# A 64 KB copy of a constant tile on SyncE's queue in front of gamma's row, in an RMSNorm-SiLU kernel

## The chip, the cores and the metric

The kernel runs on one core of one Trainium2 chip. The metric is the device time of one execution in microseconds (us), as the median of several runs. A profile is one execution recorded instruction by instruction. In it PE is the matrix engine (TensorE), DVE is VectorE, ACT is ScalarE, POOL is GpSimd, and SP is SyncE, which here does nothing but issue transfers. An engine name with a q behind it (ACTq, SPq) is that engine's sequencer issuing transfers.

## The reference

```
x: float32 [8, 1024, 2048], gamma: float32 [2048], eps = 1e-5
rms = sqrt(mean(x ** 2, axis=-1, keepdims=True) + eps)
out = gamma * x / rms
return out * (1 / (1 + exp(-out)))        # float32
```

Each of the 8192 rows of 2048 numbers is divided by its root mean square, multiplied by gamma, and put through SiLU. 67.1 MB are read and 67.1 MB are written.

## The kernel before

**Blocks.** The 8192 rows are cut into 16 blocks of 512. A block is one SBUF tile `xt` of 128 partitions with J = 4 rows each, 8192 numbers or 32 KB in a partition, 4 MB in all. Six such tiles exist (BUFS = 6), and the work is done in place: load, multiply, SiLU, store, all in the same tile. So load b can be issued only when the store of block b-6 has landed.

**Queues.** Every load of `xt` is issued by ACT (`load`, L54). Every store is issued by SP (`store`, L102). So is gamma's row (L110). In the transfer view ACT's queue is called q10 and SP's queue q1. A transfer of a 4 MB tile is 128 packets of 32 KB, one for a partition, over the 16 DMA engines, that is 8 on each, and 16 packets of 4 bytes, one for each engine, that report the end (the semaphore).

**Setup.** The order is written out by hand (`manual_schedule`), and each engine works through its own list in that order:

- ACT issues load(0); then does a Square of one column of `ones` (L109, it brings in an activation table); then issues load(1); then copies one column of `junk_v` (L116), and only then issues load(2) to load(5). L116 reads `junk_v` and, as the profile shows, comes after DVE's copy of L115.
- DVE sets `ones` (a constant tile of 128x128) and `eps_t`, then copies the broadcast gamma from PSUM to `g` (L115), and only then begins on block 0.
- SP issues the load of gamma's 8 KB into partition 0 of `g` (L110).
- PE multiplies a row of `ones` with gamma's row (L113), which puts gamma in all 128 partitions of `junk_v` in PSUM.

**Steady work.** For each block ACT and DVE share the sums of squares (`squares_scalar` L65, `squares_vector` L73), ACT takes the root (L82), DVE the reciprocal (L87). DVE then multiplies each row by it and by `g` (`multiply`, L92), and ACT applies SiLU in two halves (L98) and SP stores the block. Loads 6 to 15 are issued by ACT inside `squares_scalar`: load b+3 comes right after the first Square of block b+1.

Of the kernel before, what the change touches and what calls it, by code (L numbers as in the profile page):

```python
# [1 line left out]

# [4 lines left out]

ACT = mybir.ActivationFunctionType
ALU = mybir.AluOpType


@with_exitstack
def kernel(
    ctx: ExitStack,
    tc: tile.TileContext,
    x: bass.AP,
    gamma: bass.AP,
    eps: bass.AP,
    out: bass.AP,
):  # L20

    nc = tc.nc
    P = nc.NUM_PARTITIONS
    f32 = mybir.dt.float32
    x2 = x.flatten_outer_dims()
    o2 = out.flatten_outer_dims()  # L30
    n, d = x2.shape
    J = 4
    BUFS = 6
    nblk = n // (P * J)
    xb = x2.rearrange("(b p j) d -> b p (j d)", p=P, j=J)
    ob = o2.rearrange("(b p j) d -> b p (j d)", p=P, j=J)

    singles = ctx.enter_context(tc.tile_pool(name="singles", bufs=1))
    pool = ctx.enter_context(tc.tile_pool(name="pool", bufs=BUFS))
    small = ctx.enter_context(tc.tile_pool(name="small", bufs=2))  # L40
    psum = ctx.enter_context(tc.tile_pool(name="psum", bufs=1, space=bass.MemoryType.PSUM))

    Q = 4
    w = d // Q
    g = singles.tile([P, d], f32)
    eps_t = singles.tile([P, 1], f32)
    ones = singles.tile([P, P], f32)
    junk_a = psum.tile([P, d], f32, name="junk_a")
    junk_v = psum.tile([P, d], f32, name="junk_v")
    blocks, sss, rmss, rstds = {}, {}, {}, {}  # L50

    def load(b):
        xt = pool.tile([P, J * d], f32, name="xt")
        nc.scalar.dma_start(out=xt, in_=xb[b])  # L54
        blocks[b] = xt

    def row(b, j):
        return blocks[b][:, j * d:(j + 1) * d]

    def squares_scalar(b, loads=()):  # L60


        sss[b] = small.tile([P, J], f32, name="ss")
        for j in range(share(b)):
            nc.scalar.activation(out=junk_a, in_=row(b, j), func=ACT.Square,  # L65
                                 accum_out=sss[b][:, j:j + 1])
            if j == 0:
                for s in loads:
                    load(s)

    def squares_vector(b):
        for j in range(share(b), J):
            nc.vector.tensor_tensor_reduce(  # L73
                out=junk_v, in0=row(b, j), in1=row(b, j), scale=1.0, scalar=0.0,
                op0=ALU.mult, op1=ALU.add, accum_out=sss[b][:, j:j + 1])

    def share(b):
        return 1 if 4 <= b <= 12 and b % 2 == 0 else 2

    def root(b):  # L80
        rms = small.tile([P, J], f32, name="rms")
        nc.scalar.activation(out=rms, in_=sss.pop(b), func=ACT.Sqrt, scale=1.0 / d, bias=eps_t)  # L82
        rmss[b] = rms

    def invert(b):
        rstd = small.tile([P, J], f32, name="rstd")
        nc.vector.reciprocal(out=rstd, in_=rmss.pop(b))  # L87
        rstds[b] = rstd

    def multiply(b):  # L90
        for j in range(J):
            nc.vector.scalar_tensor_tensor(out=row(b, j), in0=row(b, j), scalar=rstds[b][:, j:j + 1],  # L92
                                           in1=g, op0=ALU.mult, op1=ALU.mult)

    def silu(b):
        for h in range(0, J, 2):
            cols = slice(h * d, (h + 2) * d)
            nc.scalar.activation(out=blocks[b][:, cols], in_=blocks[b][:, cols], func=ACT.Silu)  # L98
        store(b)

    def store(b):
        nc.sync.dma_start(out=ob[b], in_=blocks[b])  # L102

    with tc.manual_schedule():

        load(0)
        nc.vector.memset(ones, 1.0)  # L107
        nc.vector.memset(eps_t, float(eps))
        nc.scalar.activation(out=junk_a[:, 0:1], in_=ones[:, 0:1], func=ACT.Square)  # L109
        nc.sync.dma_start(out=g[0:1, :], in_=bass.AP(tensor=gamma.tensor, offset=gamma.offset, ap=[[d, 1], [1, d]]))  # L110
        for c in range(Q):
            cols = slice(c * w, (c + 1) * w)
            nc.tensor.matmul(junk_v[:, cols], ones[0:1, :], g[0:1, cols], start=True, stop=True)  # L113
        load(1)
        nc.vector.tensor_copy(out=g, in_=junk_v)  # L115
        nc.scalar.copy(out=junk_a[:, 0:1], in_=junk_v[:, d - 1:d])  # L116
        for b in range(2, BUFS):
            load(b)

        last = nblk - 1
        SOON = 3
        squares_scalar(0)
        squares_vector(0)
        root(0)
        invert(0)
        for b in range(last):
            loads = [b + 3] if BUFS <= b + 3 < nblk else []
            if b < SOON:  # L130
                multiply(b)
                squares_scalar(b + 1, loads)
                silu(b)
                squares_vector(b + 1)
                root(b + 1)
            elif b < last - 1:
                squares_scalar(b + 1, loads)
                squares_vector(b + 1)
                root(b + 1)
                multiply(b)  # L140
                silu(b)
            else:
                multiply(b)
                squares_scalar(b + 1)
                silu(b)
                squares_vector(b + 1)
                root(b + 1)
            if b + 1 < last:
                invert(b + 1)


        for j in range(J):
            if j == J // 2:
                invert(last)
            nc.vector.tensor_mul(out=row(last, j), in0=row(last, j), in1=g)  # L155
        for j in range(J):
            nc.scalar.activation(out=row(last, j), in_=row(last, j), func=ACT.Silu,  # L157
                                 scale=rstds[last][:, j:j + 1])
        store(last)


# [1 line left out]
_INS = ['x', 'gamma', 'eps']  # L163
_OUTS = [((8, 1024, 2048), 'float32')]

_NUMBERS = {'eps': 9.999999747378752e-06}


# [26 lines left out]
```

## Time and profile before

| what | value |
|---|---|
| median of 3 runs | 316.87 us (316.86 to 317.06) |
| span of the profiled execution | 315.1 us |
| moved by the DMA engines | 134.24 MB, 426 GB/s over the span |
| DVE busy | 235.3 us (75%) |
| ACT busy | 213.9 us (68%) |
| PE busy | 7.2 us (2%) |
| DMA share of the chain that ended last | 68% |

The span runs from the first to the last instruction. The device time of the runs holds it and what lies around it, 316.87 - 315.1 = 1.8 us.

### The profile page before, as it was taken

The numbers are of one execution on the slowest core, as the hardware profiler recorded it, in microseconds if no ns is written. First come the engines' busy times: TensorE is split into PE (matmuls) and PEld (weight loads), VectorE is DVE, ScalarE is ACT, GpSimd is POOL, SyncE is SP. The second block draws the span as 40 slices with busy tenths as digits, with TensorE's granted clock in tenths as the row PEclk, the third lists the DMA queues.
The fourth block names the chain that finished last, engine by engine and source line by source line (L and its number), as shares of the span: only waits on it lengthen the run. The fifth ranks groups of instructions, "written<-read, shape, count | busy, mean of one in ns | idle before, by whom it ended". The sixth has DMA issues, their size and how long they took to land.

```text
span 315.1 us, 439 instructions
## 1 busy us (share of the span) xinstructions
PE 7.2 (2%) x8; PEld 2.5 (1%) x8; DVE 235.3 (75%) x157; ACT 213.9 (68%) x137; POOL 0.2 (0%) x4
## 2 busy tenths in 40 slices
PE   6200000000000000000000000000000000000000
PEld 2000000000000000000000000000000000000000
DVE  0679697979895695957969489593995939999600
ACT  1269998972799258682687827877278768779910
POOL 0000000000000000000000000000000000000000
DMA  8999999999999999999999999999999999999997
GB/s 334 412 453 416 383 458 408 462 403 462 403 459 408 454 412 458 408 462 403 462 403 462 408 458 408 458 408 458 416 449 416 449 416 449 428 437 428 437 428 308
DMA packets 4613, 134.24 MB, mean 426 GB/s; under 512 B 514, under 2 KB 514, under 8 KB 514
## 3 DMA queue, kind: packets, MB, share of 16 engines
q10 hardware_dynamic: 2304, 67.11, 49.8%
q1 hardware_dynamic: 2306, 67.12, 49.3%
q14 instruction: 3, 0.02, 0.0%
HBM read 67.12 MB, written 67.11 MB: 426 GB/s over the span
## 4 chain that ended last, share of the span: by engine, by line
DMA 68%; DVE 14%; ACT 11%; issue 1%; ACTq 1%; DVEq 0%
DMA xt<-in_x_dram 68%; DVE xt L92 9%; DVE junk_v L73 5%; ACT xt L98 4%; ACT junk_a L65 3%; ACT xt L157 2%; ACT L82 1%; ACTq L190 1%; ACT L157 0%; ACT L98 0%; ACT rms L82 0%; DVE ss L73 0%; ACTq L54 0%; DVE rstd L87 0%; ACT L109 0%
## 5 line engine op out<-in xcount | busy, mean ns | idle before, releaser
L92 DVE SCALAR_TENSOR_TENSOR xt<-xt,rstd,g 128x2048 f32<-128x2048 f32 x60 | 137.0, 2346 | 0.1
L98 ACT ACTIVATE xt<-xt 128x4096 f32<-128x4096 f32 x30 | 108.3, 3615 | 27.4 <-DVE xt L92 27.4
L73 DVE CUSTOM_DVE_ANT_0 junk_v<-xt 128x2048 f32<-128x2048 f32 x37 | 85.1, 2299 | 42.9 <-DMA xt<-in_x_dram 42.2
L65 ACT ACTIVATE junk_a<-xt 128x2048 f32<-128x2048 f32 x27 | 50.7, 1876 | 16.1 <-DMA xt<-in_x_dram 14.0
L82 ACT ACT_TABLE_LOAD x15 | 19.2, 1283 | 26.6 <-DVE ss L73 26.5
L98 ACT ACT_TABLE_LOAD x14 | 18.0, 1283 | 0.2
L115 DVE COPY g<-junk_v 128x2048 f32<-128x2048 f32 x1 | 2.3, 2292 | 9.0 <-PE junk_v L113 9.0
L87 DVE RECIPROCAL rstd<-rms 128x4 f32<-128x4 f32 x16 | 2.7, 172 | 8.4 <-ACT rms L82 8.4
L155 DVE TENSOR_TENSOR xt<-xt,g 128x2048 f32<-128x2048 f32 x4 | 8.9, 2277 | 0.0
L82 ACT ACTIVATE rms<-ss,eps_t 128x4 f32<-128x4 f32 x16 | 4.8, 297 | 5.7 <-DVE ss L73 5.5
L157 ACT ACTIVATE xt<-xt,rstd 128x2048 f32<-128x2048 f32 x4 | 7.7, 1991 | 0.0
L113 PE MATMUL junk_v<-g,ones 1*128 1x512 f32 x8 | 7.2, 1072 | 2.8 <-DMA g<-in_gamma_dram 2.8
L116 ACT COPY junk_a<-junk_v 128x1 f32<-128x1 f32 x1 | 0.1, 144 | 9.8 <-DVE g L115 9.8
L73 DVE DVE_READ_ACCUMULATOR2_ANT ss<- 128x1 f32 x37 | 5.2, 141 | 0.0
L65 ACT ACTIVATION_READ_ACCUMULATOR junk_a<-xt 128x1 f32 x27 | 5.0, 186 | 0.0
L113 PEld LDWEIGHTS junk_v<-g,ones 1*128 1x128 f32 x8 | 2.5, 325 | 5.9 <-issue 5.9
L109 ACT ACT_TABLE_LOAD x1 | 1.3, 1283 | 1.1 <-PEq L176 1.1
L157 ACT ACT_TABLE_LOAD x1 | 1.3, 1283 | 0.0
L107 DVE MEMSET ones<- 128x128 f32 x1 | 0.2, 165 | 0.8 <-PEq L176 0.8
L109 ACT ACTIVATE junk_a<-ones 128x1 f32<-128x1 f32 x1 | 0.2, 174 | 0.0
L176 POOL MEMSET const-bfloat16-1.0<- 128x1 bf16 x1 | 0.1, 103 | 0.0
L176 POOL MEMSET const-uint8-127<- 128x1 uint8 x1 | 0.1, 102 | 0.0
(3 smaller groups left out, 0.3 us busy)
## 6 DMA issues: line engine op xcount, KB each, us to landing
xt<-in_x_dram ACTq DMA_DIRECT2D x16, 4096.0 KB, 38.7
out_dram<-xt SPq DMA_DIRECT2D x16, 4096.0 KB, 29.0
g<-in_gamma_dram SPq DMA_DIRECT2D x1, 8.0 KB
```

Source lines behind the costliest of these rows:

```text
L65: nc.scalar.activation(out=junk_a, in_=row(b, j), func=ACT.Square, accum_out=sss[b][:, j:j + 1])
L73: nc.vector.tensor_tensor_reduce(out=junk_v, in0=row(b, j), in1=row(b, j), scale=1.0, scalar=0.0, op0=ALU.mult, op1=ALU.add, accum_out=sss ...
L82: nc.scalar.activation(out=rms, in_=sss.pop(b), func=ACT.Sqrt, scale=1.0 / d, bias=eps_t)
L87: nc.vector.reciprocal(out=rstd, in_=rmss.pop(b))
L92: nc.vector.scalar_tensor_tensor(out=row(b, j), in0=row(b, j), scalar=rstds[b][:, j:j + 1], in1=g, op0=ALU.mult, op1=ALU.mult)
L98: nc.scalar.activation(out=blocks[b][:, cols], in_=blocks[b][:, cols], func=ACT.Silu)
L109: nc.scalar.activation(out=junk_a[:, 0:1], in_=ones[:, 0:1], func=ACT.Square)
L113: nc.tensor.matmul(junk_v[:, cols], ones[0:1, :], g[0:1, cols], start=True, stop=True)
L115: nc.vector.tensor_copy(out=g, in_=junk_v)
L155: nc.vector.tensor_mul(out=row(last, j), in0=row(last, j), in1=g)
L157: nc.scalar.activation(out=row(last, j), in_=row(last, j), func=ACT.Silu, scale=rstds[last][:, j:j + 1])
L190: with _tile.TileContext(nc) as tc:
```

## The change

One more SBUF tile of 128x128 float32, `spare`, and one more transfer. SP sends all of `ones`, 512 bytes in each of 128 partitions (64 KB), to `spare`, in front of gamma's row. Nothing reads `spare`. The transfer reads `ones`, which DVE sets, so SP waits for that before it issues it, and gamma's row is issued behind it by the same engine on the same queue. All other engines keep their lists of instructions.

```diff
     ones = singles.tile([P, P], f32)
+    spare = singles.tile([P, P], f32)
...
         nc.scalar.activation(out=junk_a[:, 0:1], in_=ones[:, 0:1], func=ACT.Square)
+        nc.sync.dma_start(out=spare, in_=ones)
         nc.sync.dma_start(out=g[0:1, :], in_=bass.AP(tensor=gamma.tensor, offset=gamma.offset, ap=[[d, 1], [1, d]]))
```

## The prediction

> **What bounds the kernel now.** I read the page's slices and queues first, then busy time by stretch.
>
> ```profile
> DMA  8999999999999999999999999999999999999997
> q10 hardware_dynamic: 2304, 67.11, 49.8%
> q1 hardware_dynamic: 2306, 67.12, 49.3%
> HBM read 67.12 MB, written 67.11 MB: 426 GB/s over the span
> 4.00:35.00 31.00, 5.94 (x7) 1.75 (x6) 20.95 (x14) 17.99 (x14) 0.00 (x0) 1.00 0.99 427
> 36.00:40.00 4.00, 0.00 (x0) 0.00 (x0) 3.17 (x3) 3.96 (x5) 0.00 (x0) 1.00 1.09 377
> 40.00:280.00 240.00, 0.00 (x0) 0.00 (x0) 194.53 (x129) 168.71 (x105) 0.00 (x0) 1.00 1.00 433
> ```
>
> The DMA engines are full in every slice but the first and last. The last two columns of the stretches are the DMA share and GB/s: 1.00 and 433 from 40 to 280 us. At 433 GB/s the 134.24 MB need 310.0 us of the 315.1; start, end and small dents are the rest. DVE is busy 194.5 of those 240 us, ACT 168.7. So transfers bound the kernel, and a time in which both queues are empty is lost for good. A block of 4.19 MB takes 4.19 MB / 433 GB/s = 9.7 us, so each engine's packet of 32 KB, eight to a block, takes 1.21 us.
>
> Next the timeline of the first 15 us, for what the new transfer stands in front of.
>
> ```profile
> 0.73 0.38 ACTq L54 DMA_DIRECT2D xt<-in_x_dram  x1
> 0.73 0.33 SPq L110 DMA_DIRECT2D g<-in_gamma_dram  x1
> 0.82 0.17 DVE L107 MEMSET ones<- 128x128 f32 x1 [0.82 <-PEq L176]
> 1.21 0.39 ACTq L54 DMA_DIRECT2D xt<-in_x_dram  x1
> ...
> 2.78 7.16 PE L113 MATMUL junk_v<-g,ones 1*128 1x512 f32 x8 [2.78 <-DMA g<-in_gamma_dram]
> ...
> 9.97 2.29 DVE L115 COPY g<-junk_v 128x2048 f32<-128x2048 f32 x1 [8.98 <-PE junk_v L113]
> 12.36 0.14 ACT L116 COPY junk_a<-junk_v 128x1 f32<-128x1 f32 x1 [9.75 <-DVE g L115]
> 12.38 1.81 ACTq L54 DMA_DIRECT2D xt<-in_x_dram  x4
> ```
>
> Gamma lands at 2.78. Then come eight matmuls (7.16), DVE's copy (2.29) and ACT's column, and only behind that does ACT issue loads 2 to 5, at 12.38: 9.6 us after gamma's landing. Until then loads 0 and 1 alone feed the engines. The chain of waits has load 1 from 1.21 for 21.45 us, so it lands at 22.66.
>
> **The slack.** Load 2 follows load 1 without a gap now, so it lands at 22.66 + 9.7 = 32.4. If it is issued when the queue is empty, it lands as load 0 does: the landings of L54 begin with 12.2 us from issue (shown below), so at gamma + 9.6 + 12.2. The two meet at gamma = 32.4 - 21.8 = 10.6 us. Before that a late gamma costs nothing, since loads 0 and 1 cover it; after it each us of gamma is a us in which no queue has work. The delay of the span is gamma's landing less 10.6.
>
> **How two queues share the engines.** The trace of before does not show a 64 KB copy, but shows SP's queue starting beside loads in flight: store 0, issued at 35.18. Transfer views of 35.2 to 39.55, of 40 to 45.6 and of 56.5 to 59.1 us (queue: packets, MB, share of 16 engines' time), and the landings of L54:
>
> ```profile
> q10 hardware_dynamic: 43, 1.41, 95.1%
> ...
> q1 hardware_dynamic: 34, 1.11, 46.0%
> q10 hardware_dynamic: 32, 1.05, 43.3%
> ...
> DMA packets 52, 1.18 MB, mean 454 GB/s; under 512 B 16, under 2 KB 16, under 8 KB 16
> q10 hardware_dynamic: 32, 1.05, 93.3%
> q1 hardware_dynamic: 20, 0.13, 12.0%
> ...
> DMA to landing us min/median/max: 12.2/38.7/71.5
> ```
>
> First, up to 39.55, 4.4 us after the issue, SP's queue moved nothing (q1 is not in the answer). Second, once both run, they take turns one packet each: 34 against 32. Third, a turn is a packet, whatever its size: around 58 us store 0 ends, and its 16 semaphore packets of 4 bytes come up; in that stretch the loads moved 32 packets and SP's queue these 16 and 4 large ones, 93.3% of the time against 12.0%. A packet of 4 bytes cost SP's queue its whole turn.
>
> The Trainium skill, page DMA: Bandwidth & Descriptors, section Queues, rings and completion order, says that an engine drains a whole packet from one ring before it switches, typically 9 to 17 descriptors. If its descriptors are these records, that is against the 34 to 32 above. By the rule a load's 8 and one would go as a lump; it is priced as the second rival below, from rows.
>
> **The change part by part.**
>
> *The wait for `ones`.* SP issued gamma at 0.73; now it waits for the memset, 0.82 + 0.17 = 0.99, and issues `spare` at some 1.05 and gamma 0.33 to 0.39 later (the issue rows). That is 0.7 us on gamma, hidden many times over by the 10.6 - 2.8 = 7.8 us of slack. On SP only gamma is queued behind it; the first store comes at 35 us.
>
> *The order at the engines.* Now gamma's packet goes out at 1.64 (0.9 us after its issue) and no load's packet stands in front of it. After the change load 0's packets do: they begin at about the same 1.7 to 2.8, and `spare` is issued 0.3 us behind load 0. The first turn of SP's queue, F, is bounded by two rows: below by gamma's own 0.9 us and one load packet in progress (the first ones, cold, take 1.8 us): 1.7 + 1.8 = 3.5; above by store 0's 4.4 us and the rest of a packet: 1.05 + 4.4 + 0.5 = 6.0. I take 5.5, near store 0, since it is the row with loads in flight.
>
> *The turns.* 128 packets of 512 bytes over 16 engines are 8 on each, and one semaphore packet; behind them on one engine stand gamma's 8 KB and its semaphore: 11 packets, 10 turns of the loads between them. Load 0 has some 5 packets left at F, then its own semaphore (a turn of almost nothing), then load 1's: 9 turns of 1.21 = 10.9 us. SP's own packets: eight of 512 bytes and gamma's. No row has 512 bytes; between the next ones, 4 bytes (under 0.02 us) and 8 KB (0.7 us cold), I put 0.05 each, so 0.4, and 0.5 for gamma: 0.9 together. From the last packet to the matmul 0.4 (now 1.64 + 0.7 = 2.34, and the matmul at 2.78). Gamma lands at 5.5 + 10.9 + 0.9 + 0.4 = 17.7 instead of 2.8.
>
> A table of the same page, section Bandwidth, gives 64 KB in one transfer 0.95 us when it is alone (issued from GpSimd); by it gamma would land some 2 us late and the sum would be zero. No run here shows that figure; loads in flight are what it leaves out.
>
> *What follows.* Delay = 17.7 - 10.6 = 7.1 us. Loads 2 to 5 go out at 27.3; from about 22 to 29 nothing moves. The 64 KB themselves, 8 x 0.05 = 0.4 us for each engine, lie in front of that gap and so cost nothing more.
>
> *Knock-on.* DVE and ACT start block 0 only behind `g` too, so all of their first blocks come some 14.9 us later, less the 2.75 us that ACT now waits for load 1. First store about 47 to 48, load 6 (now issued at 66.7) at about 79. Does a queue run dry? Load 5 now lands at 13.7 + 71.5 = 85.2, so load 6 has 18.5 us to spare. In the new order loads 2 to 5 run alone from 28.5 to about 52 (2.4 blocks of 9.7), the other 1.6 blocks at half pace, 31 us, to about 83: load 6 comes before that, and stores 0 to 2 are waiting beside it in any case. DVE has (240 - 194.5)/240 = 19% in hand to catch up. At the end stores are queued (store 15 lands 13.4 us after its issue, not 9.7 + start), so the transfers stay the bound. No further loss and no recovery: lost transfer time does not come back at 433 GB/s. 315.1 + 7.1 = 322.2 of span; with the 1.8 us around it, and 316.87 as the median, 324.0.
>
> Ends: F = 3.5 gives gamma 15.7 and +5.1 (322.0). F = 6.0, a tenth full turn and 0.1 us for each small packet (+0.4) give 19.8, +9.2 (326.1). A gain out of these terms is excluded: each only delays.
>
> **The rivals.**
>
> *Small packets share a turn: no change (0.10).* If the engine drains a queue's small packets together, gamma lands at 5.5 + 0.5 + 1.2 + 0.5 + 1.2 + 0.4 = 9.3, before the 10.6 that decides. Load 2 is queued in time, and only 0.4 us of packets are added: 317.3, which is within 0.2% (0.6 us, about what a measurement of this kernel can tell from no change). For it: no row has two 512-byte packets in a queue. Against it: the 4-byte packets at 58 us each took a turn.
>
> *Whole transfers take turns (0.04).* If the engines finish load 0 first and load 1 before gamma, gamma lands after 22: 22.2 - 10.6 = +11.6, 328.5. Against it: 34 to 32.
>
> *A gain (0.02).* From 36 to 40 us, as q1 starts, the engines move 377 and not 433 GB/s, a dent of 4 x 56/433 = 0.5 us. If SP's queue, once started early, no longer has it, and gamma is in time, 316.4 or somewhat less. Against it: gamma already starts that queue at 1.64 and the dent is there.
>
> **How the numbers follow.** Forecast 0.84, rivals 0.10, 0.04 and 0.02. Faster by over 0.2% 0.01, within it 0.11 (the first rival and half of the gain), slower 0.88 (the forecast and the second rival). The range 321.5 to 326.6 takes in both ends with half a us beyond, holds nearly all of the forecast's 0.84, and leaves out the rivals.
>
> **What would show it.** In the profile after: PE's wait for gamma some 15 us longer, first matmul at 15.7 to 19.8; loads 2 to 5 issued 9.6 us later; one or two of the 40 slices of DMA around 22 to 29 us with a low digit and none later; q1 with 144 more packets; steady GB/s as before. Gamma before 10.6, or late without a hole, would make it wrong, as would a second hole near 80 us or a slower steady stretch.

## The result and the profile after

The changed kernel takes 324.43 us (median of 4 runs, 324.12 to 325.65), the kernel before 316.94 beside it. The ratio is 1.0243 (95% interval 1.0226 to 1.0259). That is 7.5 us more; the forecast was 7.1 more, 324.0 us. Medians and ratios here and below are of the runs within 1.5% of the fastest of their kernel; two single runs lie above that and are named where they occur.

The transfers' part of the page of the changed kernel, 40 slices of 8.1 us each:

```profile
span 323.9 us, 440 instructions
DMA  8965999999999999999999999999999999999995
GB/s 326 428 291 190 421 425 393 445 449 417 429 449 426 421 446 437 413 445 445 405 449 445 413 437 445 421 429 449 429 421 445 445 405 445 449 405 441 449 421 243
q10 hardware_dynamic: 2304, 67.11, 48.7%
q1 hardware_dynamic: 2450, 67.18, 48.1%
```

The third and fourth slices are the new low digits (6 and 5, 291 and 190 GB/s); the last one, 5 instead of 7, comes up at the end of this section. SP's queue has 144 more packets, 128 of data and 16 semaphores. Busy time in stretches (the last two columns are the DMA share and GB/s):

```profile
4.00:22.00 18.00, 3.85 (x5) 1.79 (x6) 0.00 (x0) 0.00 (x0) 0.00 (x0) 1.00 0.98 421
22.00:28.00 6.00, 3.31 (x4) 0.69 (x3) 2.38 (x2) 0.14 (x1) 0.00 (x0) 1.00 0.00 0
54.00:290.00 236.00, 0.00 (x0) 0.00 (x0) 201.97 (x133) 176.10 (x110) 0.00 (x0) 1.00 1.00 433
320.00:322.00 2.00, 0.00 (x0) 0.00 (x0) 0.00 (x0) 0.00 (x0) 0.00 (x0) 1.00 0.12 49
```

From 22 to 28 us no data moves. Afterwards the transfers run at 433 GB/s as before, so there is no second hole. Before the hole it is 421 GB/s, against 428 in the same stretch before the change: the copy itself is hardly seen. The bytes moved up to 30 and up to 300 us say the same, first of the kernel before, then of the changed one:

```profile
DMA packets 403, 12.07 MB, mean 402 GB/s; under 512 B 34, under 2 KB 34, under 8 KB 34
DMA packets 4411, 128.67 MB, mean 429 GB/s; under 512 B 482, under 2 KB 482, under 8 KB 482
```

```profile
DMA packets 450, 8.99 MB, mean 300 GB/s; under 512 B 49, under 2 KB 177, under 8 KB 177
DMA packets 4440, 125.53 MB, mean 418 GB/s; under 512 B 481, under 2 KB 609, under 8 KB 609
```

Without the 0.07 MB of the copy, the changed kernel is 3.15 MB behind at 30 us and 3.21 MB at 300 us. At 433 GB/s that is 7.3 and 7.4 us: nearly all of the delay is there by 30 us, and hardly any comes later. The timeline of the setup shows who waits:

```profile
1.01 0.50 SPq L111 DMA_DIRECT2D spare<-ones  x1
1.57 0.64 SPq L112 DMA_DIRECT2D g<-in_gamma_dram  x1
...
18.15 7.16 PE L115 MATMUL junk_v<-g,ones 1*128 1x512 f32 x8 [18.15 <-DMA g<-in_gamma_dram]
...
25.35 2.29 DVE L117 COPY g<-junk_v 128x2048 f32<-128x2048 f32 x1 [24.36 <-PE junk_v L115]
27.73 0.14 ACT L118 COPY junk_a<-junk_v 128x1 f32<-128x1 f32 x1 [25.13 <-DVE g L117]
27.76 1.88 ACTq L55 DMA_DIRECT2D xt<-in_x_dram  x4
```

Gamma's row is issued 0.84 us later than before and lands 15.4 us later. Loads 2 to 5 still go out 9.6 us after it. In between lie the turns of the two queues; the transfer view of the changed kernel from 5 to 10 us has them:

```profile
DMA packets 122, 2.16 MB, mean 432 GB/s; under 512 B 0, under 2 KB 57, under 8 KB 57
q10 hardware_dynamic: 65, 2.13, 98.6%
q1 hardware_dynamic: 57, 0.03, 1.9%
```

In 5 us the loads moved 65 packets of 32 KB and SP's queue 57 packets of 512 bytes (its first came between 6.1 and 6.2 us), while SP's packets took 1.9% of the engines' time and the loads 98.6%. Counted from SP's first turn, from 6.1 to 15.3 us, it is packet for packet:

```profile
q10 hardware_dynamic: 144, 4.19, 105.6%
q1 hardware_dynamic: 144, 0.07, 2.4%
```

SP's 144 are all of the copy's, 128 of data and 16 semaphores; the loads' 144 are 128 packets of 32 KB and load 0's 16 semaphores.

The profiled execution took 325.65 us, the longest of the four; the other three have spans of 322.3 to 322.9. The stretch from 320 to 322 us shows where its extra us lies: a share of 0.12 of 16 engines, so one or two engines that finish after the others. The hole explains the median; it does not explain this tail.

### The profile page after: what moved, and what is told of

Its sections match the earlier page's. It is cut to its first block, busy times and chain, and to the rows that moved or that the text cites. A ratio compares the mean times of both kernels' runs of the same rounds, so it can differ in the third digit from the quotient of the medians.

```text
span 323.9 us, 440 instructions
## 1 busy us (share of the span) xinstructions
PE 7.2 (2%) x8; PEld 2.5 (1%) x8; DVE 235.0 (73%) x157; ACT 213.5 (66%) x137; POOL 0.2 (0%) x4
## 4 chain that ended last, share of the span: by engine, by line
DMA 50%; DVE 23%; ACT 13%; issue 4%; PE 2%; ACTq 1%; SPq 0%; DVEq 0%
DMA out_dram<-xt 24%; DMA xt<-in_x_dram 21%; DVE xt L93 14%; DVE junk_v L74 8%; DMA g<-in_gamma_dram 5%; ACT xt L99 5%; ACT junk_a L66 3%; PE junk_v L115 2%; ACT L83 2%; ACT xt L159 2%; DVE g L117 1%; ACTq L192 1%; ACT rms L83 1%; ACTq L55 1%; ACT L159 0%
## 6 DMA issues: line engine op xcount, KB each, us to landing
spare<-ones SPq DMA_DIRECT2D x1, 64.0 KB, 14.6
```

## The experiments

**The copy behind gamma.** The same transfer, two lines exchanged.

```diff
-        nc.sync.dma_start(out=spare, in_=ones)
         nc.sync.dma_start(out=g[0:1, :], in_=bass.AP(...))
+        nc.sync.dma_start(out=spare, in_=ones)
```

> The same 64 KB copy, but issued by SP behind gamma's row. Theory (gamma is late because the copy's packets stand in front of it): gamma lands at about 2.8 us as before the change, loads 2 to 5 go out near 12.4, no hole; the copy's packets cost 9 x 0.03 = 0.3 us for each engine at most: 316.9 to 317.3 us. Rival (the copy's 64 KB themselves, or SP's queue running beside the first loads, cost the time, wherever they stand): 324, as in the changed kernel.

317.13 us, ratio 1.001 (1.0001 to 1.0019); gamma at 2.94 us. The copy itself costs 0.2 us. The other 7.3 come from its place in front of gamma's row.

**Half of the packets, and a quarter of them.** Two kernels, with 64 and with 32 partitions:

```diff
-        nc.sync.dma_start(out=spare, in_=ones)
+        nc.sync.dma_start(out=spare[0:64, :], in_=ones[0:64, :])      # the other: 0:32
```

> The copy of 64 partitions instead of 128: 4 packets and a semaphore on each engine in front of gamma, 32 KB. Theory (one 32 KB load packet between any two of SP's): from the first turn at 6.2 us five load packets and load 0's semaphore stand between, so gamma lands at about 13.2 and the delay is 13.2 - 10.6 = 2.6 us: 319.5. Rival (delay in proportion to bytes or packets, no threshold): half of 7.5, 320.7. Rival (the small packets share a turn): gamma lands as in the changed kernel less almost nothing, 324.

> The copy of 32 partitions: two packets and a semaphore on each engine in front of gamma. Theory: four turns of 1.21 behind the first at 6.2 us, gamma at about 11.9 to 12.1, delay 1.3 to 1.5 us: 318.3. Rival (delay in proportion to the packets, no threshold): a quarter of 7.5, 318.8.

Half: gamma at 13.32 us, 319.84 us (ratio 1.0101, 1.0084 to 1.0118). Gamma fits the turns to a tenth of a us, and the delay of 2.95 is nearer to 2.6 than to the 3.8 of proportion. A quarter: gamma at 11.95 us as expected, but the time is 319.52 (1.0080, 1.0054 to 1.0106). The four runs are 318.33 to 320.76: the fastest is the expected 318.3, the others are up to 2.5 us above it. So the landing of gamma is predicted and the scatter of the end is not; this pair cannot tell a threshold from proportion by its medians.

**Four bytes instead of 512.** As many packets with a 128th of the bytes.

```diff
-        nc.sync.dma_start(out=spare, in_=ones)
+        nc.sync.dma_start(out=spare[:, 0:1], in_=ones[:, 0:1])
```

> The copy of one column: 128 packets of 4 bytes instead of 512, 0.5 KB in all. Theory (a turn is a packet, whatever its size): gamma lands at 17.9 to 18.2 us as in the changed kernel, 324.2. Rival (the bytes count): no delay worth measuring, 317.

324.29 us (1.0258, 1.0219 to 1.0297). The issue rows of the two kernels (KB, us from issue to landing), the changed one first, and then the transfer view from 5 to 10 us of the one with 4 bytes:

```profile
spare<-ones SPq DMA_DIRECT2D x1, 64.0 KB, 14.6
```

```profile
spare<-ones SPq DMA_DIRECT2D x1, 0.5 KB, 14.8
```

```profile
q10 hardware_dynamic: 68, 2.23, 103.1%
q1 hardware_dynamic: 60, 0.00, 0.7%
```

64 KB land in 14.6 us and half a KB in 14.8. Gamma lands at 17.68 us, 0.2 before the expected range. The bytes play no part that the time shows.

**The same bytes in sixteen packets.** 16 partitions of 4 KB, from one part of `g` to another. The edit is of the kernel before:

```diff
         nc.vector.memset(ones, 1.0)
+        nc.vector.memset(g[32:48, 0:8 * P], 1.0)
...
+        nc.sync.dma_start(out=g[64:80, 0:8 * P], in_=g[32:48, 0:8 * P])
         nc.sync.dma_start(out=g[0:1, :], in_=bass.AP(...))
```

> The same 64 KB in front of gamma, but as 16 partitions of 4 KB: one packet and one semaphore on each engine instead of eight and one. It goes from one part of g to another (both overwritten later), which DVE sets first with a memset of 16x1024, so SP issues it about 1 us later than in the changed kernel. Theory: first turn at 6.2 to 7.4 us, three turns of 1.21 to gamma's semaphore, so gamma at 10.5 to 12.0, delay 0 to 1.4 us: 316.9 to 318.3. Rival (64 KB in front of gamma cost it their time, however they are cut): 324.

Gamma at 12.27 us although SP issued the copy at 2.19, so 5.9 us earlier than with 512-byte packets. It lands 0.3 us after the expected range. The time is 320.40 (1.0091, 1.0069 to 1.0113), in runs of 318.67, 320.40 and 320.57, and a fourth of 324.12: the fastest is 0.4 above the upper end, the median 2.1. It speaks against the bytes, less cleanly than the run with 4 bytes.

**Twice the packets.** The same bytes as two transfers of 256 bytes of each partition:

```diff
-        nc.sync.dma_start(out=spare, in_=ones)
+        for h in range(2):
+            half = slice(h * P // 2, (h + 1) * P // 2)
+            nc.sync.dma_start(out=spare[:, half], in_=ones[:, half])
```

> The same 64 KB in two transfers of 256 bytes of each partition: 16 packets and two semaphores on each engine in front of gamma instead of eight and one. Theory (a small packet waits for a load's packet, and only as long as loads are there): all turns up to the end of load 1 at about 22.4 us are used up, then the rest goes out at once, gamma at about 22.8 to 23.3, delay 12.2 to 12.7: 329.3. Rival (each small packet takes some 1.2 us by itself, loads or not): gamma at 18.1 + 9 x 1.24 = 29.3, delay 18.7: 335.6.

330.41 us (1.0429, 1.0399 to 1.0459). From its timeline:

```profile
23.03 7.16 PE L117 MATMUL junk_v<-g,ones 1*128 1x512 f32 x8 [23.03 <-DMA g<-in_gamma_dram]
...
32.63 1.88 ACTq L55 DMA_DIRECT2D xt<-in_x_dram  x4
```

Gamma lands at 23.03, just behind the end of load 1 near 22.4, not at 29.3. So a small packet is slow only while a large one stands in the other queue. The time is 1.1 us above the expected 329.3.

**The wait alone.** The kernel before, without the copy; gamma's row waits for a memset that it overwrites.

```diff
         nc.vector.memset(eps_t, float(eps))
+        nc.vector.memset(g[0:1, 0:1], 1.0)
```

> No copy. Gamma's row only waits for DVE: a memset of one number of g (which gamma overwrites) in front of it, behind the memsets of ones and eps_t, so that SP issues gamma about 0.4 us later than before the change, behind load 0. Theory: gamma's packet now meets load 0's packets, gets its first turn near 6.2 us and its semaphore a turn later, and lands at about 8.2 instead of 2.8; that is under the 10.6 us of slack, so 316.9, no change. Rival (any lateness of gamma moves the end, without slack): 322. Rival (the wait is harmless even to gamma): gamma at about 3.2, 316.9.

Gamma is issued at 1.04 instead of 0.73 us and lands at 7.01 instead of 2.78: 0.3 us of wait cost it 4.2, because load 0 now stands in front. The time is 317.67 (1.0022, 1.0012 to 1.0031), so 0.8 us more. There is no hole, and no change was expected; most of the 4.2 us is absorbed, but not all. Its profile is of a run of 317.04 us, one of the two out of ten that were under 317.6, so it does not show where the 0.8 us lie.

**Gamma on a third queue.** The changed kernel, with gamma's row issued by GpSimd:

```diff
-        nc.sync.dma_start(out=g[0:1, :], in_=bass.AP(...))
+        nc.gpsimd.dma_start(out=g[0:1, :], in_=bass.AP(...))
```

> The changed kernel, but gamma's row is issued by GpSimd on its own queue, while SP still sends the 64 KB copy. Theory (the place behind the copy's packets is the cost): gamma has at most its own first turn and one more among the loads, and lands between 3 and 9 us, under the 10.6 of slack: 316.9 to 317.7, with 0.2 of that for the copy's packets. Rival (any small transfer that meets the first loads is held up by the same 15 us, whatever its queue): gamma near 18, 324.

317.30 us (1.0014, 1.0005 to 1.0023), gamma at 8.40. The copy is sent at the same time as in the changed kernel; gamma no longer stands behind it. The row also travels differently: on GpSimd's queue (q0) it is 16 packets of 512 bytes and 16 semaphores, 32 records, and not one packet of 8 KB and one semaphore. That is still one packet and one semaphore for each engine. Queue position is the cost, and this is a cure that keeps the copy in its place.

**The loads before the wait.** The changed kernel, with loads 2 to 5 moved in front of ACT's wait for `g`:

```diff
         load(1)
+        for b in range(2, BUFS):
+            load(b)
         nc.vector.tensor_copy(out=g, in_=junk_v)
         nc.scalar.copy(out=junk_a[:, 0:1], in_=junk_v[:, d - 1:d])
-        for b in range(2, BUFS):
-            load(b)
```

> The changed kernel, but ACT issues loads 2 to 5 right after load 1, before its copy of junk_v's column that waits for g. Gamma stays late. Theory (the loss is the hole between load 1 and load 2, not gamma's lateness in itself): gamma at 18.1 as in the changed kernel, no hole at 22 to 28 us; 316.9 and 0.2 for the copy's packets. DVE and ACT still begin 15 us late, and all six tiles are loaded by about 67 us, before stores free them: the transfers may run dry near 80 us, where load 6 waits for ACT, for 1 to 3 us. So 317.1 to 320. Rival (the late start of DVE and ACT is the loss): 324, no change against the changed kernel.

321.04 us (1.0123, 1.0095 to 1.0151), in five runs of 319.28 to 322.50 and a sixth of 327.32. Neither theory has this number. Stretches of its profile, and the last line from the kernel before:

```profile
22.00:28.00 6.00, 3.16 (x4) 0.66 (x2) 2.54 (x2) 0.39 (x2) 0.00 (x0) 1.00 1.01 437
78.00:82.00 4.00, 0.00 (x0) 0.00 (x0) 2.30 (x4) 2.90 (x4) 0.00 (x0) 1.00 0.97 418
100.00:104.00 4.00, 0.00 (x0) 0.00 (x0) 4.00 (x3) 3.97 (x4) 0.00 (x0) 1.00 1.02 371
313.00:318.00 5.00, 0.00 (x0) 0.00 (x0) 0.00 (x0) 0.00 (x0) 0.00 (x0) 1.00 0.29 125
...
313.00:314.00 1.00, 0.00 (x0) 0.00 (x0) 0.00 (x0) 0.00 (x0) 0.00 (x0) 1.00 0.01 0
```

The hole is filled (437 GB/s from 22 to 28), gamma still lands at 18.00, and 3.4 us of the 7.5 are won back. But 4.1 us remain (4.2 with the sixth run). They are not a dry spell near 80 us, as I had thought: the share there is 0.97. Some 2 us are lost all the same between 60 and 120 us, where 25.28 MB are moved against 26.17 before the change, 0.89 MB less, with a share that stays near 1 (371 GB/s from 100 to 104 us). The rest is at the end: after 313 us, where the kernel before is done, the share is 0.29 for 5 us. Most engines are done, and a few still work off their packets.

**The same order without the copy.** The kernel before, with loads 2 to 5 moved as above.

> The kernel before, without the copy, but with loads 2 to 5 issued right behind load 1, as in the run with the loads before the wait. Gamma at 2.8 us. It tells apart what is left of the loss in that run (4.2 us, with no hole at 22 to 28 us but engines that end unevenly between 312 and 319 us). Theory (what is left comes from DVE and ACT starting 15 us late, with all six tiles loaded before the first store): here they start on time, 316.9. Rival (six loads queued from the start make the engines drift apart whatever gamma does): about 320 to 321.

317.03 us (1.0003, 0.9993 to 1.0012). Six loads queued from the start do no harm by themselves, so the 4.1 us need the copy in front of gamma too. The copy by itself costs 0.2 us, which leaves late gamma, and with it late DVE and ACT, as the likely cause; the wait alone points the same way (gamma 4.2 us late without a copy or a hole, 0.8 us). A late gamma with six loads queued and no copy was not run, and how late work slows the transfers and makes the engines end unevenly was not settled. No version that was run is faster than the kernel before.

## Why the prediction was right

**The bound.** Transfers fill every slice, so a time in which both queues are empty stays lost. It held: 6 us at a share of 0.00, then 433 GB/s as before, and 7.3 of the 7.5 us lost by 30 us.

**The slack of 10.6 us.** Delay is gamma's landing less 10.6. Over all runs that shift gamma and leave the loads behind it (landing, measured median, and 316.9 plus the excess over 10.6):

| kernel | gamma lands | measured | by the rule |
|---|---|---|---|
| copy behind gamma | 2.94 | 317.13 | 316.9 |
| wait alone | 7.01 | 317.67 | 316.9 |
| third queue | 8.40 | 317.30 | 316.9 |
| a quarter | 11.95 | 319.52 (from 318.33) | 318.3 |
| sixteen packets | 12.27 | 320.40 (from 318.67) | 318.6 |
| half | 13.32 | 319.84 | 319.6 |
| 4 bytes | 17.68 | 324.29 | 324.0 |
| changed kernel | 18.15 | 324.43 | 324.5 |
| twice | 23.03 | 330.41 (from 329.35) | 329.3 |

Gamma's landing is right to 0.5 us for the changed kernel (17.7 forecast) and for each kernel whose packets were counted. The wait alone, put at 8.2, landed 1.2 us earlier; its first turn came one load packet sooner (below). The rule of the slack gives half the packets, 4 bytes and the changed kernel to 0.3 us, and twice the packets to 1.1. From the wait alone to the sixteen packets, around the threshold, the medians lie 0.4 to 1.8 us above it, with a wide scatter for the last two, and that excess is not explained: the profiles of a quarter and of the sixteen packets are of runs of 318.66 and 318.67 us, which do not have it.

**The terms of gamma's landing.** The first turn was put at 5.5, between 3.5 and 6.0; it came at 6.1 to 6.2, 5.1 us after SP's issue, so a little beyond the row of store 0 (4.4) that I had leaned on, and beyond the upper end. That wait is no fixed time from the issue: the copy of sixteen packets, issued at 2.19, had its first turn at the same 6.1 to 6.2, and gamma's row alone, issued at 1.04, at 5.0 to 5.1. By then 48 to 49 packets of load 0 had begun for the copies, three for each engine, and 34, some two for each, for gamma's row. Why two in one case and three in the other is open. A packet of 512 bytes was put at 0.05 us; 57 of them took 1.9% of 16 engines in 5 us, 16 x 5 x 0.019 / 57 = 0.027. The two misses partly cancel. The turns, which carry most of the sum, were counted rightly.

**The rule on arbitration.** The Trainium skill, DMA: Bandwidth & Descriptors, Queues, rings and completion order, has an engine drain a packet of typically 9 to 17 descriptors before it changes the ring. If a record here is a descriptor, this case differs: 65 to 57, and 68 to 60 with 4 bytes, are turns of one. By lumps of that size gamma would have landed behind load 1, after 22 us, for 328.5, which is the prediction's estimate for its second rival; it landed at 18.15, and the measurement decides. The table's 0.95 us for 64 KB, which the prediction calls the time alone, stands there for loads from HBM, with no word on other transfers of the same core; beside the loads the copy took 14.6 us.

**The rivals.** A shared turn of small packets is refuted by the 144 to 144 from 6.1 to 15.3 us, turns of whole transfers by them too. A gain from an early start of SP's queue is not seen: the run with the copy behind gamma is 0.2 us longer, not shorter.

**What was off.** I held that the late start of DVE and ACT costs nothing. In the changed kernel no loss shows from that between 54 and 290 us, but the run with the loads before the wait shows that this holds only behind the hole: with the hole filled, 4.1 us are lost elsewhere, some 2 of them between 60 and 120 us and the rest in uneven ends.

## What to carry to other kernels

Count the packets for each DMA engine in front of a small urgent transfer on its queue, and multiply by the time of one packet of the other queue, not by their own size: with eight packets of 27 ns and a semaphore in front, gamma's row landed 11.1 us later beside loads in packets of 32 KB (18.15 against 7.01 with the wait alone), of which some 10 are turns (eight load packets of 1.21 us and its own small ones) and the rest is a first turn one load packet later. Put the urgent row first, or on a queue of its own, and cut what must stand in front into few packets. How late it may be is read from the moment at which the work already queued runs out.

## What the runs showed of the hardware

- Two queues take turns packet by packet, whatever the size: 144 records against 144 from the first turn to the copy's last semaphore with packets of 32 KB and of 512 bytes, and 68 against 60 in 5 us with 4 bytes. A semaphore takes a turn too.
- A queue that starts beside loads in flight is slow to its first turn: 5.1 us from the issue of the copy, 4.4 for the first store, 4.0 for gamma's row in the wait alone, 3.9 for the sixteen packets. The copies had it at 6.1 to 6.2 us whether issued at 1.01 or at 2.19. At an idle start gamma took 0.9.
- SP took 0.50 us to issue the copy and 0.64 for gamma behind it; gamma alone took 0.33.
- The 16 engines need not end together: with late DVE and ACT work and six loads queued they spread over some 5 us (share 0.29 from 313 to 318 us, against 0.01 from 313 to 314 before). What spreads them was not found.
